# Windowed attention: queries turned raw, divided out inside the exponent; keys turned as whole numbers

## The chip, the cores and the metric

One of the cores of a Trainium2 chip runs the whole program in one launch. The metric is the device time of that launch in microseconds (us). A run of the hardware profiler gives, beside it, the span from the first to the last instruction of the program; the two differ by a little under 2 us. TensorE is called PE here, its weight loads PEld, VectorE DVE, ScalarE ACT, GpSimd POOL, and the engine that issues DMAs SP.

## The reference, cut to what matters

One encoder layer is computed for 1280 tokens (1024 of one request, 256 of another) of width 2048: a norm, a wide projection, three groups of heads side by side (a two-way state space scan, a windowed attention, a cross attention to a memory), and an output projection. The change lies in the windowed attention alone. It has eight query heads of 64, two key heads, blocks of 128 tokens, and a window of one block to either side:

```python
q = rms_norm(q.reshape(b, T, ATT_HEADS, ATT_HEAD_DIM), q_norm_g)
k = rms_norm(k.reshape(b, T, ATT_KV_HEADS, ATT_HEAD_DIM), k_norm_g)
...
s = jnp.einsum('bnqgrd,bnkgd->bngrqk', qb, kw).astype(jnp.float32) * (d ** -0.5)
...
logits = jnp.where(valid[:, None, None], s - slopes[None, :, :, None, None] * dist[:, None, None], -jnp.inf)
sk = sink.astype(jnp.float32).reshape(KV, r)[:, :, None, None]
m = jnp.maximum(jnp.max(logits, axis=-1, keepdims=True), sk)
pr = jnp.exp(logits - m)
probs = pr / (jnp.sum(pr, axis=-1, keepdims=True) + jnp.exp(sk - m))
o = jnp.einsum('bngrqk,bnkgd->bnqgrd', probs.astype(v.dtype), vw)
```

The norm of a query divides a whole row of logits by one positive number. With r the reciprocal root of a query's mean square, exp(r*s - slope*dist - m) is the same as exp(r*(s - (slope/r)*dist) - m).

## The kernel before, in words

**Precision.** Every large matmul takes its operands in fp32r. A number x is split in two, a high part h that ACT writes by a copy into an fp32r tile, and a low part x - h that DVE writes. Three matmuls (h·h, h·l, l·h) then stand for one. These triples over 512, 288 or 320 columns (lines 254 to 256, 289 to 291, 1199 to 1201) accumulate in five PSUM banks of the pool "acc". They are called the stream here. For every tile of weights that arrives, ACT makes wh (line 202) and DVE wl (line 203).

**The lanes.** What is not in the stream (attention, scan, preparation of keys) is written as Python generators that yield after each step. They wait in two queues, lanes 0 and 1. After each k of a projection the function `pump` takes steps from both lanes at a rate given in RATES (in the second group of tokens some 1.6 steps of lane 0 and 2.5 of lane 1 for each k). The keys' `k_prep`, the windowed attention's `attn` and the cross attention's `mem_attn` are in lane 0, the scan in lane 1. A scheduler then orders the instructions of each engine by dependences and priorities; weight splits and evacuations stand ahead (`high_priority`). All steps share three PSUM banks of the pool "mix" (`psum(name)`), one after the other: a tile takes the bank of the third tile before it, and PE waits until that has been read. They also share a ring of five SBUF tiles called "wa" (`w2`).

**k_prep(t)**, ten times: a block's keys (128 tokens, two heads of 64) are loaded, normed on DVE (lines 488 and 489), split into a high and a low part, each written twice side by side (lines 493 and 495), turned by four fp32r transposes (line 501), and copied out of PSUM into kT by DVE (line 504) and kL by ACT (line 505). Both halves of kT's 128 partitions hold the same high parts, and both of kL's the same low parts.

**attn(t)**, ten times: the block's queries q (128 by 512) are loaded (line 593); ACT squares them, DVE adds up per head (line 598), POOL makes r by a power of -1/2 (`rsqrt`, lines 120 and 121); DVE multiplies q by r (line 604). For each of the two key heads ACT and DVE write the four query heads' high and low parts side by side into qh (lines 610 and 611), PE turns them by four transposes (line 616), ACT copies them to a tile qT (line 618), whose partitions 0 to 63 hold the high and 64 to 127 the low parts. So one matmul with kT and one with kL (lines 632 and 633) give the logits of a head. Then, in `scores`, DVE adds the slope times the distance (line 634), takes the row's maximum with the sink (lines 637 to 641), ACT takes the exponent (line 647) and DVE divides (line 652); `turn_` turns the probabilities (line 664), `values` multiplies them with v (line 674).

`mem_attn` already turns its queries unscaled and gives r to its exponent (lines 720 to 746).

Of the kernel before, what the change touches and what calls it, by code (L numbers as in the profile page):

```python
# [10 lines left out]
F32 = mybir.dt.float32  # L11
F32R = mybir.dt.float32r
# [3 lines left out]
AF = mybir.ActivationFunctionType  # L16
ALU = mybir.AluOpType
AX = mybir.AxisListType

P = 128  # L20
# [8 lines left out]
CH, WB, RB, WA, WBB = 4, 3, 4, 5, 4  # L29
# [14 lines left out]
def hymba_encoder_kernel(  # L44
# [7 lines left out]
    V, A, G, T, S = nc.vector, nc.scalar, nc.gpsimd, nc.tensor, nc.sync  # L52
# [14 lines left out]
    sm = ctx.enter_context(tc.tile_pool(name="sm", bufs=2))  # L67
# [8 lines left out]
    def const(shape, name, dtype=F32):  # L76
        return cp.tile(shape, dtype, tag=name, name=name)
# [4 lines left out]
    def psum(name):  # L82
        return mix.tile([P, 512], F32, tag="mix", name=name)


    identr = const([P, P], "identr", F32R)
    ident = identr.bitcast(F32)
# [2 lines left out]
    ones = one.broadcast_to([P, P])  # L90
    mhalf = const([P, 16], "mhalf")
    V.memset(mhalf, -0.5)

    whole = rp.tile([P, 640], F32, tag="ch", name="whole", bufs=CH)[:, :P]
    make_identity(nc, whole)
# [23 lines left out]
    def rsqrt(dst, src, scale, n):  # L119
        G.tensor_scalar(out=dst, in0=src, scalar1=scale, scalar2=EPS, op0=ALU.mult, op1=ALU.add)  # L120
        G.tensor_tensor(out=dst, in0=dst, in1=mhalf[:, :n], op=ALU.pow)

    def hv(ap, n=8):
        return ap.rearrange("p (h d) -> p h d", h=n)

    def hb(ap, n, d):
        return ap.unsqueeze(2).broadcast_to([P, n, d])
# [283 lines left out]
    def w2(name):  # L411
        return mp.tile([P, 512], F32, tag="wa", name=name, bufs=WA)
# [63 lines left out]
    def k_prep(t):  # L476
        r = w2("kr")[:, :P]
        S.dma_start(r, k_d[t])
        yield
        ss = sm.tile([P, 2], F32, tag="s2", name="kss", bufs=4)  # L480
        sq = w2("ksq")[:, :P]
        A.activation(sq, r, AF.Square)
        V.reduce_sum(out=ss, in_=hv(sq, 2), axis=AX.X)
        rr = sm.tile([P, 2], F32, tag="s2", name="krr", bufs=4)
        rsqrt(rr, ss, 1.0 / 64, 2)
        yield
        r3 = hv(r, 2)
        V.tensor_mul(r3, r3, hb(rr, 2, 64))
        V.tensor_mul(r3, r3, gq.unsqueeze(1).broadcast_to([P, 2, 64]))

        kh = mp.tile([P, 4, 2, 64], F32R, tag="wa", name="kh", bufs=WA)
        for d in range(2):
            A.activation(kh[:, 0:2, d, :], r3, AF.Copy)
        for d in range(2):
            V.tensor_sub(kh[:, 2:4, d, :], r3, kh[:, 0:2, 0, :].bitcast(F32))
        yield
        yield
        ps = psum("pk")
        kf = kh.rearrange("p a b d -> p (a b d)")
        for a in range(4):  # L500
            T.transpose(ps[:, a * P:(a + 1) * P].bitcast(F32R), kf[:, a * P:(a + 1) * P], identr)
        sl = t if t < 5 else t - 3
        c = slice(sl * P, (sl + 1) * P)
        V.tensor_copy(kT[:, :, c], hv(ps[:, :256], 2))
        A.activation(kL[:, :, c], hv(ps[:, 256:], 2), AF.Copy)
        yield

    def kv_shift():
# [74 lines left out]
    def attn(t):  # L583
# [3 lines left out]
        nk = na * P  # L587
        d0 = (k0 - (t - 1)) * P
        s0 = k0 if t < 4 else k0 - 3
        grp, ti = divmod(t, 5)  # L590
        tc_ = slice(ti * P, (ti + 1) * P)
        q = w2("q")
        S.dma_start(q, q_d[t])
        yield
        sq = w2("sq")
# [2 lines left out]
        V.reduce_sum(out=ss, in_=hv(sq), axis=AX.X)  # L598
        r = sm.tile([P, 8], F32, tag="s8", name="qr", bufs=4)
        rsqrt(r, ss, 1.0 / 64, 8)  # L600
        for _ in range(3):
            yield
        q3 = hv(q)
        V.tensor_mul(q3, q3, hb(r, 8, 64))
        yield
        qT = []
        for b in range(2):
            qh = mp.tile([P, 4, 2, 64], F32R, tag="wa", name="qh", bufs=WA)
            qb = q3[:, 4 * b:4 * b + 4, :]
            A.activation(qh[:, :, 0, :], qb, AF.Copy)  # L610
            V.tensor_sub(qh[:, :, 1, :], qb, qh[:, :, 0, :].bitcast(F32))
            yield
            ps = psum("pq")
            qf = qh.rearrange("p a b d -> p (a b d)")
            for a in range(4):
                T.transpose(ps[:, a * P:(a + 1) * P].bitcast(F32R), qf[:, a * P:(a + 1) * P], identr)
            o = mp.tile([P, 512], F32R, tag="qT", name="qT", bufs=2)
            A.activation(o, ps, AF.Copy)
            qT.append(o)
        z = w2("za")  # L620
        S.dma_start(hv(z, 4), zT_d[0][grp][:, :, tc_])
        yield
        sk8 = sinkb.rearrange("p (v r) -> p r v", v=2)
        state_ = {}

        def scores(rr):
            lg = mp.tile([P, 2, 384], F32, tag="lg", name="lg", bufs=2)
            for kv in range(2):
                h = 4 * kv + rr
                ps = psum("psc")  # L630
                st = qT[kv][:, rr * P:(rr + 1) * P]
                T.matmul(ps[:, :nk], st, kT[:, kv, s0 * P:s0 * P + nk], start=True, stop=False)
                T.matmul(ps[:, :nk], st, kL[:, kv, s0 * P:s0 * P + nk], start=False, stop=True)
                V.scalar_tensor_tensor(out=lg[:, kv, :nk], in0=ndist[:, d0:d0 + nk], scalar=2.0 ** -(h + 1),
                                       in1=ps[:, :nk], op0=ALU.mult, op1=ALU.add)
            m = sm.tile([P, 2], F32, tag="m2", name="m", bufs=10)
            V.reduce_max(out=m, in_=lg[:, :, :nk], axis=AX.X)
            sk = sk8[:, rr, :]
            nm = sm.tile([P, 2], F32, tag="m2", name="nm", bufs=10)
            V.tensor_max(m, m, sk)  # L640
            V.tensor_scalar(out=nm, in0=m, scalar1=-1.0, scalar2=None, op0=ALU.mult)
            es = sm.tile([P, 2], F32, tag="m2", name="es", bufs=10)
            V.tensor_add(es, sk, nm)
            A.activation(es, es, AF.Exp)
            den = sm.tile([P, 2], F32, tag="m2", name="den", bufs=10)
            for kv in range(2):
                A.activation(lg[:, kv, :nk], lg[:, kv, :nk], AF.Exp, bias=nm[:, kv:kv + 1],
                             accum_out=den[:, kv:kv + 1])
            V.tensor_add(den, den, es)
            V.reciprocal(out=den, in_=den)  # L650
            for kv in range(2):
                V.tensor_scalar(out=lg[:, kv, :nk], in0=lg[:, kv, :nk], scalar1=den[:, kv:kv + 1], scalar2=0.5,
                                op0=ALU.mult, op1=ALU.mult)
            state_[rr] = lg
# [24 lines left out]
        scores(0)  # L679
        yield  # L680
        scores(1)
        yield
        yield
# [818 lines left out]
    mp = beside.enter_context(tc.tile_pool(name="mp", bufs=2))  # L1502
# [3 lines left out]
    kT = lconst([P, 2, 7 * P], "kT", F32R)  # L1506
    kL = lconst([P, 2, 7 * P], "kL", F32R)
# [12 lines left out]
    ndist = lconst([P, 384], "ndist", BF16)  # L1520
    gq, gm = lconst([P, 64], "gq"), state[:, :P]
    dskip, sinkb = lconst([P, 16], "dskip"), lconst([P, 8], "sinkb")
# [158 lines left out]
```

## Time and profile before

| | |
|---|---|
| runs shown | 1801.31, 1802.39 and 1802.70 us, median 1802.39 |
| the profiled execution, its own time | 1802.42 us |
| its span | 1800.7 us |
| PE busy | 1791.2 us, 10546 matmuls |
| DVE, ACT, POOL busy | 1244.3, 903.0 and 439.5 us |
| granted TensorE clock | 1.00 |
| first and last turning of queries | 552.5 and 1317.0 us |

PE is at work nearly throughout. "Busy" counts a matmul from its start to its modelled end, and neighbours overlap: a 128x512 matmul of the stream is listed with some 0.39 us, while the next one starts 0.23 us after it. What a matmul costs the program is the time from its start to the next one's start, and a view in order of time gives that.

### The profile page before, as it was taken

How to read it: one execution, taken by the hardware profiler on the slowest of the kernel's cores; microseconds unless marked ns; L12 is line 12 of the kernel's file. 1: busy time of each engine (PE TensorE's matmuls, PEld its weight loads, DVE VectorE, ACT ScalarE, POOL GpSimd, SP SyncE). 2: the span in 40 equal slices, each digit the busy share in tenths (PEclk: the TensorE clock that was granted, in tenths of full speed). 3: DMA queues.
4: the chain of work that ended last, by engine and by line, in shares of the span. 5: the costliest groups of instructions: out<-in, count | busy, mean ns of one | idle time of the engine just before them, and what ended most of it. 6: DMA issues, size and time to landing. Idle time of an engine off the chain costs nothing.

```text
span 1800.7 us, 30423 instructions
## 1 busy us (share of the span) xinstructions
PE 1791.2 (99%) x10546; PEld 1606.1 (89%) x10546; DVE 1244.3 (69%) x2422; ACT 903.0 (50%) x2039; POOL 439.5 (24%) x714
## 2 busy tenths in 40 slices
PE   9999999999999999999999999999999999999999
PEld 7789999999887899999989987887898888889999
DVE  5595788877657978775755866666885654866665
ACT  6554455444445756564435646544574533543332
POOL 0105789961110000000000000001100000058775
PEclk9999999999999999999999999999999999999999
DMA  8664455446544644444436355457785564644442
GB/s 291 198 179 120 138 153 146 129 136 218 164 136 147 184 134 140 121 132 134 119 96 192 110 161 180 128 178 235 231 266 168 184 190 138 216 153 147 142 143 80
DMA packets 198891, 290.58 MB, mean 161 GB/s; under 512 B 18960, under 2 KB 80464, under 8 KB 198736
## 3 DMA queue, kind: packets, MB, share of 16 engines
q1 hardware_dynamic: 198592, 288.57, 52.7%
q8 instruction: 83, 1.36, 0.3%
q14 instruction: 72, 0.59, 0.1%
q10 hardware_dynamic: 144, 0.06, 0.0%
HBM read 231.12 MB, written 57.44 MB: 160 GB/s over the span
## 4 chain that ended last, share of the span: by engine, by line
PE 61%; DVE 1%; ACT 1%; issue 1%; DMA 1%; POOL 0%; POOLq 0%; ACTq 0%; DVEq 0%
PE acc L254 9%; PE acc L256 8%; PE acc L255 8%; PE acc L289 5%; PE acc L291 5%; PE acc L290 5%; PE acc L1199 3%; PE acc L1201 3%; PE acc L1200 3%; PE py L931 2%; PE po L674 1%; PE ppt L664 1%; PE accm L1200 1%; PE accm L1201 1%; PE accm L1199 1%
## 5 line engine op out<-in xcount | busy, mean ns | idle before, releaser
L203 DVE TENSOR_TENSOR wl<-wraw,wh 128x512 fp32r<-128x512 f32 (+1 forms) x480 | 338.9, 708 | 241.3 <-ACT wh L202 230.7
L254 PE MATMUL acc<-wh,xH 128*128 128x512 f32 (+1 forms) x1248 | 481.9, 386 | 0.2 <-ACT mkr L416 0.2
L255 PE MATMUL acc<-wl,xH 128*128 128x512 f32 (+1 forms) x1248 | 472.2, 378 | 0.9 <-DVE wl L203 0.6
L256 PE MATMUL acc<-wh,xL 128*128 128x512 f32 (+1 forms) x1248 | 472.8, 379 | 0.0
L202 ACT ACTIVATE wh<-wraw 128x512 fp32r<-128x512 f32 (+1 forms) x480 | 292.4, 613 | 323.5 <-PE acc L256 173.3
L254 PEld LDWEIGHTS acc<-wh,xH 128*128 128x128 f32 x1248 | 234.5, 188 | 45.1 <-issue 4.8
L255 PEld LDWEIGHTS acc<-wl,xH 128*128 128x128 f32 x1248 | 234.7, 188 | 43.8 <-DVE wl L203 3.3
L256 PEld LDWEIGHTS acc<-wh,xL 128*128 128x128 f32 x1248 | 234.2, 188 | 43.9 <-issue 0.9
L289 PE MATMUL acc<-xH,wh 128*128 128x320 f32 x640 | 204.5, 320 | 0.0
L291 PE MATMUL acc<-xH,wl 128*128 128x320 f32 x640 | 198.6, 310 | 0.0
L290 PE MATMUL acc<-xL,wh 128*128 128x320 f32 x640 | 198.3, 310 | 0.0
L203 DVE TENSOR_TENSOR sl<-ws,sh 128x384 fp32r<-128x384 f32 x144 | 99.6, 695 | 96.9 <-ACT sh L202 96.6
L202 ACT ACTIVATE sh<-ws 128x384 fp32r<-128x384 f32 x144 | 74.6, 523 | 176.5 <-POOL ws L1171 81.5
L1171 POOL TENSOR_TENSOR ws<-wraw 128x128 f32<-128x128 f32 x144 | 91.1, 633 | 202.0 <-DMA wraw<-in_w_in_pairs_dram 83.6
L289 PEld LDWEIGHTS acc<-xH,wh 128*128 128x128 f32 x640 | 120.3, 188 | 4.1 <-issue 3.7
L290 PEld LDWEIGHTS acc<-xL,wh 128*128 128x128 f32 x640 | 120.3, 188 | 2.6 <-issue 2.2
L291 PEld LDWEIGHTS acc<-xH,wl 128*128 128x128 f32 x640 | 120.1, 188 | 0.7 <-issue 0.6
L1171 POOL TENSOR_TENSOR ws<-wraw,ws 128x128 f32<-128x128 f32 x144 | 93.5, 649 | 11.3
L358 DVE SCALAR_TENSOR_TENSOR c<-u,vec,c 128x638 f32<-128x638 f32 (+1 forms) x96 | 88.6, 926 | 10.0 <-ACT c L353 9.7
L1171 POOL TENSOR_TENSOR ws<-ws,wraw 128x128 f32<-128x128 f32 x144 | 94.2, 654 | 0.0
L120 POOL TENSOR_SCALAR qr<-qss 128x8 f32<-128x8 f32 x10 | 4.3, 428 | 366.6 <-DVE qss L598 366.6
L1171 POOL TENSOR_TENSOR wraw<-wraw 128x128 f32<-128x128 f32 x144 | 89.2, 620 | 11.1
(427 smaller groups left out, 3645.1 us busy)
## 6 DMA issues: line engine op xcount, KB each, us to landing
wraw<-in_w_in_laid_dram SPq DMA_DIRECT2D x208, 256.0 KB, 2.8
wraw<-in_w_in_pairs_dram SPq DMA_DIRECT2D x80, 256.0 KB, 2.8
wraw<-in_w_out_laid_dram SPq DMA_DIRECT2D x64, 256.0 KB, 3.5
wraw<-in_w_out_pairs_dram SPq DMA_DIRECT2D x64, 256.0 KB, 2.8
rf<-ac SPq DMA_DIRECT2D x40, 256.0 KB, 3.7
rb<-ac SPq DMA_DIRECT2D x40, 256.0 KB, 4.1
wraw<-in_w_mem_laid_dram SPq DMA_DIRECT2D x32, 256.0 KB, 4.8
xst<-in_x_sample_dram SPq DMA_DIRECT2D x20, 256.0 KB, 4.7
```

The lines of the kernel that those rows point to most:

```text
L202: a = A.activation(h, raw, AF.Copy)
L203: b = V.tensor_sub(l, raw, h.bitcast(F32))
L254: T.matmul(ps[t][:, :n], sh, h[:, :n], start=(k_ == 0), stop=False)
L255: T.matmul(ps[t][:, :n], sh, l[:, :n], start=False, stop=False)
L256: T.matmul(ps[t][:, :n], sl, h[:, :n], start=False, stop=(k_ == KT - 1))
L289: T.matmul(o, sh, cur["H", q][:, m, c], start=(k == 0), stop=False)
L290: T.matmul(o, sh, cur["L", q][:, m, c], start=False, stop=False)
L291: T.matmul(o, sl, cur["H", q][:, m, c], start=False, stop=(k == KT - 1))
L358: V.scalar_tensor_tensor(out=c[0], in0=u[:, k:k + n], scalar=cw[k], in1=c[0], op0=ALU.mult, op1=ALU.add)
L1171: G.tensor_tensor(out=o, in0=x, in1=y, op=op)
L1199: T.matmul(ps[p], h, xh, start=(k_ == 0), stop=False)
L1200: T.matmul(ps[p], h, xl, start=False, stop=False)
```

## The change

Keys: the normed block is written twice side by side in fp32 and turned by two transposes in fp32, not split before. DVE then copies the high part out of PSUM into kT and subtracts it from PSUM into kL; ACT's copy into kL is gone.

Queries: the raw block is turned as it was loaded, four transposes instead of eight. Each now holds two neighbouring heads, the even one in partitions 0 to 63, the odd one in 64 to 127. For either half ACT copies the high part into a tile qT at the same partitions, and DVE writes the low part into the other half of that tile. The multiplication by r is gone. In its place DVE makes 1/r, slope/r and sink/r (three instructions of 8 columns), the slope of line 634 becomes a column, the maximum is multiplied by -r, and the exponent's scale is r, a column too. A constant tile of eight slopes is set at the start by eight memsets.

`attn` now yields nine times ahead of its first scores, and eight times before: 22 steps in all against 21. `k_prep` has as many as it had.

```diff
+    slope = const([P, 8], "slope")
+    for h in range(8):
+        V.memset(slope[:, h:h + 1], 2.0 ** -(h + 1))
...
-        kh = mp.tile([P, 4, 2, 64], F32R, tag="wa", name="kh", bufs=WA)
+        k2 = mp.tile([P, 2, 2, 64], F32, tag="wa", name="k2", bufs=WA)
         for d in range(2):
-            A.activation(kh[:, 0:2, d, :], r3, AF.Copy)
-        for d in range(2):
-            V.tensor_sub(kh[:, 2:4, d, :], r3, kh[:, 0:2, 0, :].bitcast(F32))
+            A.activation(k2[:, :, d, :], r3, AF.Copy)
         yield
         yield
         ps = psum("pk")
-        kf = kh.rearrange("p a b d -> p (a b d)")
-        for a in range(4):
-            T.transpose(ps[:, a * P:(a + 1) * P].bitcast(F32R), kf[:, a * P:(a + 1) * P], identr)
+        for a in range(2):
+            T.transpose(ps[:, a * P:(a + 1) * P], k2[:, a].rearrange("p d c -> p (d c)"), ident)
...
         V.tensor_copy(kT[:, :, c], hv(ps[:, :256], 2))
-        A.activation(kL[:, :, c], hv(ps[:, 256:], 2), AF.Copy)
+        V.tensor_sub(kL[:, :, c], hv(ps[:, :256], 2), kT[:, :, c].bitcast(F32))
...
-        q = w2("q")
+        qr = mp.tile([P, 512], F32R, tag="wa", name="q", bufs=WA)
+        q = qr.bitcast(F32)
...
         rsqrt(r, ss, 1.0 / 64, 8)
-        for _ in range(3):
+        yield
+        yield
+        ps = psum("pq")
+        for a in range(4):
+            T.transpose(ps[:, a * P:(a + 1) * P].bitcast(F32R), qr[:, a * P:(a + 1) * P], identr)
+
+        qT = [mp.tile([P, 512], F32R, tag="qT", name="qT", bufs=2) for _ in range(2)]
+        for b in range(2):
+            x, y = slice(64 * b, 64 * b + 64), slice(64 - 64 * b, 128 - 64 * b)
+            A.activation(qT[b][x], ps[x], AF.Copy)
+            V.tensor_sub(qT[b][y], ps[x], qT[b][x].bitcast(F32))
             yield
-        q3 = hv(q)
-        V.tensor_mul(q3, q3, hb(r, 8, 64))
-        yield
-        qT = []
-        for b in range(2):
-            qh = mp.tile([P, 4, 2, 64], F32R, tag="wa", name="qh", bufs=WA)
-            qb = q3[:, 4 * b:4 * b + 4, :]
-            A.activation(qh[:, :, 0, :], qb, AF.Copy)
-            V.tensor_sub(qh[:, :, 1, :], qb, qh[:, :, 0, :].bitcast(F32))
-            yield
-            ps = psum("pq")
-            qf = qh.rearrange("p a b d -> p (a b d)")
-            for a in range(4):
-                T.transpose(ps[:, a * P:(a + 1) * P].bitcast(F32R), qf[:, a * P:(a + 1) * P], identr)
-            o = mp.tile([P, 512], F32R, tag="qT", name="qT", bufs=2)
-            A.activation(o, ps, AF.Copy)
-            qT.append(o)
+        yield
+
+        ri = sm.tile([P, 8], F32, tag="s8", name="qri", bufs=4)
+        V.reciprocal(out=ri, in_=r)
+        slr, skr = [sm.tile([P, 8], F32, tag=n, name=n, bufs=1) for n in ("slr", "skr")]
+        V.tensor_mul(slr, ri, slope)
+        V.tensor_mul(skr, ri, sinkb)
+        yield
+        yield
...
-                st = qT[kv][:, rr * P:(rr + 1) * P]
+                st = qT[rr % 2][:, h // 2 * P:(h // 2 + 1) * P]
...
-                V.scalar_tensor_tensor(out=lg[:, kv, :nk], in0=ndist[:, d0:d0 + nk], scalar=2.0 ** -(h + 1),
+                V.scalar_tensor_tensor(out=lg[:, kv, :nk], in0=ndist[:, d0:d0 + nk], scalar=slr[:, h:h + 1],
...
-            V.tensor_max(m, m, sk)
-            V.tensor_scalar(out=nm, in0=m, scalar1=-1.0, scalar2=None, op0=ALU.mult)
+            V.tensor_max(m, m, skr8[:, rr, :])
+            V.scalar_tensor_tensor(out=nm, in0=m, scalar=-1.0, in1=r8[:, rr, :], op0=ALU.mult, op1=ALU.mult)
...
-                A.activation(lg[:, kv, :nk], lg[:, kv, :nk], AF.Exp, bias=nm[:, kv:kv + 1],
+                h = 4 * kv + rr
+                A.activation(lg[:, kv, :nk], lg[:, kv, :nk], AF.Exp, scale=r[:, h:h + 1], bias=nm[:, kv:kv + 1],
```

How the instructions move. Line numbers of the changed program are three to four higher than before. The first place is PE's order at the first block's queries, before (L616 turns qh into the bank pq, L254 to L256 are the stream):

```order
L255 MATMUL acc<-wl,xH_1178 128x512
L256 MATMUL acc<-wh,xL_1179 128x512
L616 MATMUL pq<-identr,qh 128x128 x8
L254 MATMUL acc<-wh,xH_859 128x512
L255 MATMUL acc<-wl,xH_859 128x512
```

The same place of the changed program (L606 turns q, L935 is a matmul of the scan in lane 1, L257 to L259 are the stream):

```order
L259 MATMUL acc<-wh,xL_1188 128x512
L935 MATMUL py<-xs,rb 128x64 x8
L606 MATMUL pq<-identr,q 128x128 x4
L257 MATMUL acc<-wh,xH_1187 128x512
L258 MATMUL acc<-wl,xH_1187 128x512
```

Two groups of four have become one, it comes some 28 rows earlier, and here it follows another short group directly.

The second place is DVE's order at the same block, before (qss is the sum of squares from which POOL makes qr; wl is the low part of a weight tile; ya and zs belong to other work):

```order
L598 TENSOR_REDUCE qss<-sq 128x8
L203 TENSOR_TENSOR wl<-wraw,wh 128x512
L934 TENSOR_TENSOR ya<-xs,dco 128x512
L504 CAST kT<-pk 128x2x128
L203 TENSOR_TENSOR wl<-wraw,wh 128x512 x2
L604 TENSOR_TENSOR q<-q,qr 128x512
L611 TENSOR_TENSOR qh<-q,qh 128x4x64 x2
L203 TENSOR_TENSOR wl<-wraw,wh 128x512
```

and now:

```order
L599 TENSOR_REDUCE qss<-sq 128x8
L206 TENSOR_TENSOR wl<-wraw,wh 128x512
L938 TENSOR_TENSOR ya<-xs,dco 128x512
L504 CAST kT<-pk 128x2x128
L206 TENSOR_TENSOR wl<-wraw,wh 128x512
L505 TENSOR_TENSOR kL<-pk,kT 128x2x128
L206 TENSOR_TENSOR wl<-wraw,wh 128x512
L617 RECIPROCAL qri<-qr 128x8
L619 TENSOR_TENSOR slr<-qri,slope 128x8
L620 TENSOR_TENSOR skr<-qri,sinkb 128x8
L206 TENSOR_TENSOR wl<-wraw,wh 128x512
L941 TENSOR_TENSOR ya<-ya,py 128x512
```

The first instruction that needs POOL's qr is now the reciprocal, six instructions behind the sum instead of five; the two subtractions out of pq follow a few rows further on.

The third place is PE's order at the queries of the ninth block (t = 8), with the buffers' numbers. Before, right behind the two groups of transposes and thirty matmuls of the stream (psc is a head's logits, pyb a matmul of the scan's way back):

```order
L632 MATMUL psc_14383<-kT_4805,qT_14295 128x256
L633 MATMUL psc_14383<-kL_4806,qT_14295 128x256
L632 MATMUL psc_14387<-kT_4805,qT_14320 128x256
L633 MATMUL psc_14387<-kL_4806,qT_14320 128x256
L1029 MATMUL pyb_14408<-state_4813,cc_14301 128x512
L632 MATMUL psc_14418<-kT_4805,qT_14295 128x256
L633 MATMUL psc_14418<-kL_4806,qT_14295 128x256
L632 MATMUL psc_14422<-kT_4805,qT_14320 128x256
L633 MATMUL psc_14422<-kL_4806,qT_14320 128x256
```

and now, at the transposes themselves (pr is a turning of the scan's output, L292 to L294 the stream):

```order
L606 MATMUL pq_14295<-identr_84,q_14172 128x128 x4
L1033 MATMUL pyb_14308<-state_4822,cc_14224 128x512
L997 MATMUL pr_14317<-identr_84,yd_14092 128x128 x4
L292 MATMUL acc_14346<-xH0_6769,wh_14352 128x320
L293 MATMUL acc_14346<-xL0_6770,wh_14352 128x320
L294 MATMUL acc_14346<-xH0_6769,wl_14353 128x320
L292 MATMUL acc_14347<-xH0_6769,wh_14352 128x320
L293 MATMUL acc_14347<-xL0_6770,wh_14352 128x320
L1033 MATMUL pyb_14325<-state_4822,cc_14224 128x512
```

Before, five tiles of the pool "mix" followed one another directly at the scores; now pyb_14325 is the third tile behind pq_14295, so it takes pq's bank, five matmuls of the stream behind pr.

More of the change, by code (lines that the diff above doesn't have):

```diff
@@ L622, in attn @@
         yield
-        sk8 = sinkb.rearrange("p (v r) -> p r v", v=2)
+        sk8, skr8, r8 = [x.rearrange("p (v r) -> p r v", v=2) for x in (sinkb, skr, r)]
         state_ = {}
```

## The prediction

> **What bounds the kernel now.** I read the page first: the busy shares, then the chain that ended last.
>
> ```profile
> span 1800.7 us, 30423 instructions
> ...
> PE 1791.2 (99%) x10546; PEld 1606.1 (89%) x10546; DVE 1244.3 (69%) x2422; ACT 903.0 (50%) x2039; POOL 439.5 (24%) x714
> ...
> PE 61%; DVE 1%; ACT 1%; issue 1%; DMA 1%; POOL 0%; POOLq 0%; ACTq 0%; DVEq 0%
> ```
>
> PE is idle for 9.5 us of 1800.7, and no other engine has more than 1% of the chain. To see whether that also holds where the windowed attention runs (queries are turned from 552 to 1317 us), I cut the span in three.
>
> ```profile
> 0.00:480.00 480.00, 477.14 (x2796) 438.91 (x2797) 348.85 (x576) 242.59 (x480) 229.95 (x367) 1.00 0.56 170
> 480.00:1360.00 880.00, 878.00 (x5221) 770.43 (x5220) 628.78 (x1387) 480.30 (x1206) 50.53 (x77) 1.00 0.53 160
> 1360.00:1801.00 441.00, 436.05 (x2532) 396.73 (x2531) 266.69 (x460) 180.07 (x356) 159.02 (x270) 1.00 0.50 154
> ```
>
> The columns are the stretch, its length, then PE, PEld, DVE, ACT and POOL busy, the granted clock, the DMAs. In the middle stretch PE is idle for 2.0 us of 880, DVE for 251, ACT for 400. So there the end is moved by two things: matmul time added or taken away, and any new wait of PE. Work on DVE, ACT and POOL counts only if PE comes to wait for it.
>
> **Turned queries.** What a short group costs is the time from its start until the stream has its pace again. PE in order of time at the first queries, then at a key block, then at a turning of the memory's keys, which is one in fp32:
>
> ```profile
> 552.50 0.80 PE L616 MATMUL pq<-identr,qh 128*128 128x128 f32 x8
> 553.13 0.47 PE L254 MATMUL acc<-wh,xH 128*128 128x512 f32 x1
> 553.44 0.40 PE L255 MATMUL acc<-wl,xH 128*128 128x512 f32 x1
> ```
> ```profile
> 494.94 0.40 PE L859 MATMUL pst<-fh,btl 128*128 128x512 f32 x1
> 495.17 0.46 PE L501 MATMUL pk<-identr,kh 128*128 128x128 f32 x4
> 495.48 0.46 PE L254 MATMUL acc<-wh,xH 128*128 128x512 f32 x1
> 495.78 0.40 PE L255 MATMUL acc<-wl,xH 128*128 128x512 f32 x1
> ```
> ```profile
> 441.35 0.60 PE L444 MATMUL pmk<-identr,mkr 128*128 128x128 f32 x4
> 441.71 0.48 PE L254 MATMUL acc<-wh,xH 128*128 128x512 f32 x1
> 442.02 0.39 PE L255 MATMUL acc<-wl,xH 128*128 128x512 f32 x1
> ```
>
> A matmul of the stream takes 0.23 us from start to start (494.94 to 495.17). From the group's start to L255's start, less that one, are 0.94 - 0.23 = 0.71 us for eight transposes in fp32r, 0.61 - 0.23 = 0.38 for four, 0.67 - 0.23 = 0.44 for four in fp32. In all three the L254 behind the group takes some 0.31 instead of 0.23, so 0.08 belongs to the break itself. In PE's order before, the 80 transposes of queries stand as four groups of eight and twelve of four: 4 x 0.71 + 12 x 0.38 = 7.4 us. Now there are ten groups of four, 3.8. **The queries give back 3.6 us.**
>
> **Turned keys.** Ten groups of four in fp32r at 0.38 become ten groups of two in fp32; half of 0.44 is 0.22. **The keys give back 10 x 0.16 = 1.6 us.** The two matmuls of a head's logits keep their number and shape.
>
> **Breaks.** With the queries read earlier, the scheduler sets other short groups side by side. Counting along PE's order, the stream is taken up again behind a transpose, a value matmul or a matmul of the scan's diagonal 143 times before and 127 times now; one of the sixteen is a pq and already counted. 15 x 0.08 = **1.2 us less.** Bounds: nothing, if the wait behind a longer group eats it, and 2.4 us, if a group's front costs as much as its back.
>
> **The start.** DVE sets eight slopes between mhalf and zero, and zero is what the first matmuls wait for.
>
> ```profile
> 0.86 0.06 DVE L89 MEMSET one<- 128x1 f32 x1 [0.86 <-PEq L1667]
> 0.90 0.07 DVE L92 MEMSET mhalf<- 128x16 f32 x1
> 0.97 0.27 DVE L1460 MEMSET zero<- 128x256 f32 x1
> ```
> ```profile
> 1.30 4.64 PE L1462 MATMUL warm<-zero 128*128 128x256 f32 x10 [1.30 <-DVE zero L1460]
> 5.37 0.84 PE L254 MATMUL acc<-wh,xH 128*128 128x512 f32 x1
> ```
>
> A memset's successor starts 0.04 to 0.07 us after it, so the ten warm-up matmuls start 0.3 to 0.6 us later, and the first of the stream is issued while they still run. **0.3 us more**, by the 128x1 row; nothing, if the first operands are as late.
>
> **The other engines.** The rows by line and shape:
>
> ```profile
> L604 DVE TENSOR_TENSOR q<-q,qr 128x512 f32<-128x512 f32 x10 | 6.9, 686 | 1.8 <-POOL qr L121 1.8
> L611 DVE TENSOR_TENSOR qh<-q,qh 128x256 fp32r<-128x256 f32 x20 | 8.1, 419 | 1.0 <-ACT qh L610 1.0
> L724 DVE TENSOR_TENSOR mql<-pmq,mqh 128x512 fp32r<-128x512 f32 x10 | 6.8, 685 | 0.9 <-ACT mqh L722 0.9
> L640 DVE TENSOR_TENSOR m<-m,sinkb 128x2 f32<-128x2 f32 x40 | 6.2, 155 | 0.2
> L495 DVE TENSOR_TENSOR kh<-kr,kh 128x128 fp32r<-128x128 f32 x20 | 4.9, 286 | 3.9 <-ACT kh L493 3.9
> L504 DVE CAST kT<-pk 128x256 fp32r<-128x256 f32 x10 | 4.2, 423 | 8.9 <-PE pk L501 8.9
> ```
> ```profile
> L618 ACT ACTIVATE qT<-pq 128x512 fp32r<-128x512 f32 x20 | 11.4, 590 | 2.8 <-PE pq L616 2.8
> L610 ACT ACTIVATE qh<-q 128x256 fp32r<-128x256 f32 x20 | 7.6, 407 | 6.0 <-DVE q L604 6.0
> L505 ACT ACTIVATE kL<-pk 128x256 fp32r<-128x256 f32 x10 | 3.8, 376 | 2.1 <-DVE kT L504 1.7
> L746 ACT ACTIVATE mpr<-pms,mm,mr 128x256 f32<-128x256 f32 x40 | 22.2, 560 | 23.0 <-DVE mm L742 23.0
> L647 ACT ACTIVATE lg<-lg,nm 128x256 f32<-128x256 f32 x32 | 16.0, 502 | 13.9 <-DVE nm L641 13.9
> ```
>
> DVE, for a query block: 0.69 + 2 x 0.42 = 1.52 go; two subtractions of 512 columns out of PSUM come (0.685 each, L724 is the like) and three of 8 columns at 0.155: 1.84. For a key block two of 0.286 go, one like L504 at 0.42 comes. Over ten blocks +3.2 and -1.5: 1.7 us more, under DVE's 251 idle ones. ACT loses 20 x 0.407 and 3.8 us. Its exponent takes r as a column; L746, which has that already, takes 560 ns for 256 columns where L647 takes 502, though it reads PSUM: 80 x 0.058 = 4.6 us more. In sum ACT has 7.3 us less. All of it is covered by PE, at nothing.
>
> For that column the Trainium skill, ScalarE: Activation LUTs, section What ACT_TABLE_LOAD costs, has a price that speaks against the change: each [128,1] pointer operand adds about 93 ns to an ACTIVATE. By it the exponents would grow by an estimated 7.4 us instead of 4.6; the rows' 58 ns compare two sources, so this trace neither confirms nor excludes 93.
>
> The reciprocal waits for POOL's qr. Behind it on DVE stand weight splits, for which the stream waits. In DVE's order six instructions lie between the sum and it, five before, so the 1.8 us that L604 waited in all ten blocks do not grow. Ready queries come five steps before their scores and no longer one: PE's weight loads waited 1.5 us for qT and PE itself 0.2, and I take the **0.2 as gain**, 1.5 at most.
>
> ```profile
> PE psc L632 <- ACT qT L618: 0.2, 1, 0.2
> ...
> PE ppt L664 <- DVE lg L652: 0.9, 2, 0.5
> ```
> ```profile
> PEld psc L632 <- ACT qT L618: 1.5, 4, 0.6
> ```
>
> Queries' loads keep their number and SP its stream of weight loads; with four tiles of the "wa" ring to a block in place of six, no load finds its tile taken for longer. The added step of attn pushes lane 0 back by up to six k. The lane still empties in the same loop, and the scan's last step is the last to end in both, and the added step holds no instruction of its own, so it costs nothing.
>
> **The bank pq.** Before, one ACT copy (0.59 us) freed it. Now ACT, DVE beside ACT, DVE must have read it: 0.59 + 0.69 + 0.69 = 2.0 us at least. PE feels it only when the third tile of the pool "mix" comes within that time. The closest is the ninth block, with two pyb matmuls, pr and five of the stream between: some 2 us by the chain's rows.
>
> ```profile
> 1304.69 0.86 PE pyb L1029 x2
> ```
>
> The bounds are nothing and ten times the added 1.4, 14 us. mem_attn reads its bank by ACT and DVE already, and no row of PE's waits has more than 1.3 us. I take **0.5 us more**.
>
> **Sum**: -3.6 - 1.6 - 1.2 + 0.3 - 0.2 + 0.5 = -5.8 us. The profiled execution took 1802.42 (span and 1.7 around it), the median is 1802.39. **Forecast 1796.6 us.** A measurement of this kernel tells 0.2% from no change, 3.6 us: faster is below 1798.8, slower above 1806.0.
>
> **Rivals.**
> First, a longer chain behind the scores: with 58 ns more in both exponents of all 40 pairs of heads, `turn_` finds its probabilities later, and PE waits at ppt. If PE took all of it, 4.6 us: 1801.2, no change to be told. For it speaks that PE does wait for lg (0.9 us above); against it that these are two waits out of 80.
> The skill's 93 ns would make this rival's time an estimated 1804.0, no change either.
> Second, the other side: the bank pq. If subtractions queue behind evacuations and splits on DVE, the bank is held longer in every block, in-order PE stops, and the stream behind it. From 0.94 us a block it is slower by over 0.2%; with 1.4 us in each, instead of the 0.5 in all, 1796.6 + 13.5 = 1810.1. For it: three banks for two lanes. Against it: in nine of ten blocks the third tile is further off.
> Third, more than forecast: breaks at 2.4, the 1.5 of the weight loads, no wait for pq, start hidden: -3.6 - 1.6 - 2.4 - 1.5 = -9.1, 1793.3. For it: five score tiles in a row at the ninth block are pulled apart. Against it: waits that go often reappear elsewhere.
>
> **How the numbers follow.** Forecast 0.55, first rival 0.14, second 0.09, third 0.22. The forecast's own range is 1794 to 1799.5; with the first and third rival the range is 1791.5 to 1802, and the pq case stays outside. Faster: all of the third, most of the forecast's share, little of the first: 0.72. Within 0.2%: 0.19. Slower: 0.09.
>
> **What would show it.** Right: PE with 60 matmuls less (10486), its busy time down by some 5 us and its idle time still near 9.5; L606 as ten groups with 0.38 us each; pk as ten groups with 0.22; ACT with 7 us less, DVE about as before. Wrong: rows of PE waiting for DVE qT or ACT qT (second rival), or for DVE lg (first); a pk group that costs as much in fp32 with two as with four before would take 1.6 us of the sum; a subtraction into the other 64 partitions well over 0.7 us would lengthen the hold of pq.

## The result, and the profile after

| | before | after |
|---|---|---|
| median of 11 runs each, us | 1802.70 (1801.25 to 1806.17) | 1806.67 (1804.74 to 1809.44) |
| ratio, 95% interval | | 1.0021 [1.0013, 1.0029] |
| the profiled execution, its own time, us | 1802.42 | 1806.20 |
| PE idle in the span, us | 9.5 | 15.6 |

The changed kernel is 4 us slower, where 5.8 us less were forecast. The page of the profile after, its span, its busy shares and the chain that ended last:

```profile
span 1804.3 us, 30282 instructions
...
PE 1788.7 (99%) x10486; PEld 1602.8 (89%) x10486; DVE 1256.7 (70%) x2440; ACT 898.4 (50%) x2009; POOL 434.6 (24%) x714
...
PE 84%; DMA 5%; issue 5%; DVE 3%; ACT 2%; SPq 1%; POOL 0%; ACTq 0%; DVEq 0%; POOLq 0%
```

PE has its 60 matmuls less and its busy time fell by 2.5 us (some 5 were forecast), but its idle time grew by 6.1. DMA, ACT and DVE had 3% of the chain before and have 10% now. What PE waited for, as engine, line, tile, releaser: us in total, times, longest:

```profile
PE ppt L668 <- DVE lg L656: 2.7, 1, 2.7
PE warm L1466 <- DVE zero L1464: 1.5, 1, 1.5
PE psc L635 <- DVE lg L637: 1.2, 1, 1.2
PE pr L997 <- ACT pT L669: 1.1, 1, 1.1
PE pst L861 <- ACT pT L669: 1.0, 1, 1.0
PE pst L861 <- ACT fh L875: 0.9, 1, 0.9
PE pst L862 <- DVE fl L883: 0.9, 1, 0.9
```

No row waits for qT, so the bank pq is not it. Six waits are new at this size; one of pst for pT, 1.0 us, ends at 1086 us, the five others, 6.8 us, lie between 1269 and 1352. Busy time by stretch there, of the kernel before and then of the changed one (the columns are those of the prediction):

```profile
1260.00:1360.00 100.00, 99.09 (x627) 87.66 (x627) 83.81 (x194) 63.62 (x164) 8.37 (x16) 1.00 0.81 249
```
```profile
1260.00:1360.00 100.00, 93.01 (x582) 82.28 (x581) 80.72 (x182) 59.38 (x148) 6.36 (x14) 1.00 0.73 230
```

PE is idle for 7.0 us of these 100 and was for 0.9. Setting the starts of the same matmul of the stream side by side in both traces, the changed kernel is 5.0 us ahead at 1293 us and 2.2 us behind at 1357 us. So the changed kernel had a lead, and lost more than that in 64 us. The lead is no measure of the gain: part of it is work of lane 0, which stands later here (by how much is counted below), that was still to be done. ACT in order of time in the changed kernel shows how (L199 splits a load of the output stage's operand, L651 is the exponent of the tenth query block; the number in brackets is the idle time before a row and what ended it):

```profile
1341.48 0.82 ACT L199 ACTIVATE xH<-chd,vec 128x640 fp32r<-128x640 f32 x1
1347.47 0.83 ACT L199 ACTIVATE xH<-chd,vec 128x640 fp32r<-128x640 f32 x1 [5.17 <-DMA chd<-oT]
...
1348.82 0.59 ACT L651 ACTIVATE lg<-lg,nm,qr 128x256 f32<-128x256 f32 x1
...
1363.45 0.59 ACT L651 ACTIVATE lg<-lg,nm,qr 128x256 f32<-128x256 f32 x1
```

and DVE and then PE right behind it (L656 divides the exponents, L668 turns them):

```profile
1350.12 0.16 DVE L653 TENSOR_TENSOR den<-den,es 128x2 f32<-128x2 f32 x1 [0.57 <-ACT lg L651]
...
1351.62 0.60 DVE L656 TENSOR_SCALAR lg<-lg,den 128x256 f32<-128x256 f32 x2
```
```profile
1348.96 0.39 PE L257 MATMUL acc<-wh,xH 128*128 128x512 f32 x1
1352.01 0.70 PE L668 MATMUL ppt<-identr,lg 128*128 128x128 f32 x4 [2.66 <-DVE lg L656]
```

The first and the last of this block's eight large exponents are shown; all eight come behind a split at which ACT stands for 5.17 us, since its load has not landed and ACT takes its instructions in order. The load is not a slow one: it was issued at 1342.24 us, when ACT was just about to come to it, and landed in 5.2 us; the twelve loads of this tile between 1300 and 1360 us have a median of 4.5 us here and 4.8 in the kernel before. DVE's den, its product and PE's turning wait in line. The four smaller waits in the stretch (psc, pr and the two pst) were not followed to their ends. In the kernel before, the same eight ran from 1321 to 1346 us, before the split that waits:

```profile
1321.37 0.51 ACT L647 ACTIVATE lg<-lg,nm 128x256 f32<-128x256 f32 x1
...
1345.68 0.50 ACT L647 ACTIVATE lg<-lg,nm 128x256 f32<-128x256 f32 x1
...
1352.18 0.83 ACT L196 ACTIVATE xH<-chd,vec 128x640 fp32r<-128x640 f32 x1 [0.86 <-DMA chd<-oT]
```

Why they came later now: counted in the program, the tenth block's 21 steps stood at the k from 333 to 354 of 383, its 22 stand at 341 to 358. Each block has one more step, which takes a turn of the lane, and the loads of the output stage's operand start at fixed k, from 339 on.

### The profile page after: what moved, and what is told of

It is laid out like the page before. It is cut to its first block, busy times and chain, and to the rows that moved or that the text cites. A ratio compares the mean times of both kernels' runs of the same rounds, so it can differ in the third digit from the quotient of the medians.

```text
span 1804.3 us, 30282 instructions
## 1 busy us (share of the span) xinstructions
PE 1788.7 (99%) x10486; PEld 1602.8 (89%) x10486; DVE 1256.7 (70%) x2440; ACT 898.4 (50%) x2009; POOL 434.6 (24%) x714
## 4 chain that ended last, share of the span: by engine, by line
PE 84%; DMA 5%; issue 5%; DVE 3%; ACT 2%; SPq 1%; POOL 0%; ACTq 0%; DVEq 0%; POOLq 0%
PE acc L257 11%; PE acc L259 11%; PE acc L258 11%; PE acc L1205 6%; PE acc L1203 6%; PE acc L1204 6%; PE acc L292 5%; PE acc L293 5%; PE acc L294 5%; PE accm L1203 2%; PE accm L1204 2%; PE accm L1205 2%; PE py L935 2%; PE po L678 1%; PE ppt L668 1%
## 5 line engine op out<-in xcount | busy, mean ns | idle before, releaser
L257 PE MATMUL acc<-wh,xH 128*128 128x512 f32 (+1 forms) x1248 | 481.4, 386 | 0.4 <-DVE v_all L336 0.4
L259 PE MATMUL acc<-wh,xL 128*128 128x512 f32 (+1 forms) x1248 | 473.3, 379 | 0.0
L257 PEld LDWEIGHTS acc<-wh,xH 128*128 128x128 f32 x1248 | 234.5, 188 | 44.7 <-issue 3.2
L259 PEld LDWEIGHTS acc<-wh,xL 128*128 128x128 f32 x1248 | 234.3, 188 | 44.0 <-issue 1.3
L292 PE MATMUL acc<-xH,wh 128*128 128x320 f32 x640 | 201.5, 315 | 0.0
L294 PE MATMUL acc<-xH,wl 128*128 128x320 f32 x640 | 199.2, 311 | 0.0
L292 PEld LDWEIGHTS acc<-xH,wh 128*128 128x128 f32 x640 | 120.2, 188 | 2.4 <-issue 2.0
L294 PEld LDWEIGHTS acc<-xH,wl 128*128 128x128 f32 x640 | 120.2, 188 | 1.6 <-issue 1.6
```

The source lines that it names most:

```text
L257: T.matmul(ps[t][:, :n], sh, h[:, :n], start=(k_ == 0), stop=False)
L259: T.matmul(ps[t][:, :n], sl, h[:, :n], start=False, stop=(k_ == KT - 1))
L292: T.matmul(o, sh, cur["H", q][:, m, c], start=(k == 0), stop=False)
L294: T.matmul(o, sl, cur["H", q][:, m, c], start=False, stop=(k == KT - 1))
```

## The experiments

Three theories at first. A: the added step costs, by moving the last blocks into those loads. B: the exponents, longer by the column, hold up what follows (the prediction's first rival). C: the bank pq is held (its second).

**The step alone: taken from the change, and given to the kernel before.**

```diff
 the change
-            yield
             yield
 
         ri = sm.tile([P, 8], F32, tag="s8", name="qri", bufs=4)
```
```diff
 the kernel before
             qT.append(o)
+        yield
         z = w2("za")
```

> The changed kernel with the one yield taken out that stands alone behind the two splits of the queries, so that attn has 21 steps as before and every unit of lane 0 stands at the same k as before; all operations are the changed ones. Theory A (the added step moves the ninth and tenth block and what follows in lane 0 into the refill of the next operand, where ACT waits for that refill's loads with exponents queued behind): the stalls of PE between 1290 and 1360 us go, and the time is 1797 us, 5 to 6 below the kernel before. Theory B (the longer exponent, 88 to 92 ns more in each of 80, makes PE wait at the turned probabilities): still slower than before, near 1806. Theory C (the bank pq is held by four readers): still slower than before, 1803 to 1806.

> The kernel before with one empty yield added in attn ahead of the load of za: 22 steps, all operations as before. Theory A: slower than before by the stalls alone, 6 to 9 us, 1809 to 1812 us, with ACT waiting some 5 us for a chd load near 1345 us and PE for lg behind it. Theories B and C: as before, within 2 us of it.

Without the step 1802.25 us (11 runs), ratio to the kernel before 0.9999 [0.9991, 1.0008]: by the ratios 4.0 us less than the change, but not below the kernel before, so the 1797 that theory A gave did not come. With the step alone 1808.71 (6 runs), 1.0036 [1.0024, 1.0048]: an empty step costs 6.3 us, with no change to the work at all. Its ACT waits for the same loads, though not for 5 us at one of them as was expected; the stretch, then what ACT waited for:

```profile
1260.00:1360.00 100.00, 96.29 (x611) 86.50 (x609) 80.65 (x180) 60.12 (x152) 7.93 (x14) 0.98 0.77 241
```
```profile
ACT xH L196 <- DMA chd<-oT: 5.0, 4, 1.9
```

In the changed kernel this row reads:

```profile
ACT xH L199 <- DMA chd<-oT: 7.1, 3, 5.2
```

PE's longest wait in the kernel with the step alone is not for lg either, but for the bank pq (pst takes the bank that the copy L618 to qT has to free), and the granted clock is at half behind that wait:

```profile
PE pst L858 <- ACT qT L618: 3.5, 1, 3.5
```
```profile
1341.00:1342.00 1.00, 1.00 (x3) 0.75 (x3) 1.00 (x3) 1.00 (x3) 0.00 (x0) 0.50 0.99 218
```

The copy, at 1338.16 us, comes behind splits on ACT that stood for their loads 1.90, 0.86 and 0.52 us, and behind other work of ACT. From 1339.6 to 1343.3 us the stream's matmuls start up to 0.43 us apart and not 0.23, which loses some 1.6 us. With the 2.8 us that PE is idle more in this stretch, that is 4.4 of the 5.7 us by which the two profiled spans differ. The mean granted clock is 0.998 or 0.999 in all six runs of this kernel and 1.000 in all 29 of the kernel before beside them. In the changed kernel it is 0.999 in five of eleven runs, whose median is 1807.92 us, and 1.000 in the other six, with 1805.8. So part of the price can be a slower clock behind a wait; the trace of the change, taken at 1.000, does not hold it.

**The exponent's column alone, and the keys alone, in the kernel before.** `one` is a column of ones.

```diff
-                A.activation(lg[:, kv, :nk], lg[:, kv, :nk], AF.Exp, bias=nm[:, kv:kv + 1],
+                A.activation(lg[:, kv, :nk], lg[:, kv, :nk], AF.Exp, scale=one, bias=nm[:, kv:kv + 1],
```

> The kernel before, whose 80 exponents of the windowed attention take a column of ones as their scale in place of the constant 1: the output stays what it was, and each exponent reads one more column. All theories: ACT's exponents rise from 606 and 502 ns to some 698 and 590, 7 us of ACT in all. Theory B: 4 to 7 us slower than before, 1807 to 1810. Theories A and C: within 1.5 us of before.

> The kernel before with the changed preparation of the keys alone (turned in fp32 by two transposes, low part subtracted out of PSUM by DVE); queries as before. All theories: ten groups of PE at 0.22 instead of 0.38 us, 1.6 us less, 1801; the scheduler may move that by 1 us. If two fp32 transposes cost as much as four in fp32r, as before.

With the column 1802.19 (11 runs), 1.0003 [0.9994, 1.0011], and not 4 to 7 us more: theory B falls. The exponents did grow, all 80, and were covered:

```profile
L647 ACT ACTIVATE lg<-lg,nm,one 128x384 f32<-128x384 f32 x48 | 33.5, 699 | 20.1 <-DVE nm L641 20.1
L647 ACT ACTIVATE lg<-lg,nm,one 128x256 f32<-128x256 f32 x32 | 18.9, 592 | 12.2 <-DVE nm L641 12.1
```

The keys' part of the diff alone: 1800.66 (11 runs), 0.9992 [0.9983, 1.0000], 1.4 us of a forecast 1.6, with an interval from nothing to 3.1.

**Is it the step or the place?** The change keeps its step, and lane 0 gets 22/21 of its rate in the second group's projections, so that the tenth block stands at 332 to 354 again.

```diff
-         {'kv': (1.2, 1.5), 'x': (1.75, 1.85), 'q': (1.6, 2.5), 'za': (1.6, 2.5), 'z0': (1.55, 2.6),
-          'z1': (1.55, 2.65), 'mq': (1.55, 2.8), 'zm': (1.55, 2.85), 'o': (1.95, 1.9)})
+         {'kv': (1.2, 1.5), 'x': (1.75, 1.85), 'q': (1.676, 2.5), 'za': (1.676, 2.5), 'z0': (1.624, 2.6),
+          'z1': (1.624, 2.65), 'mq': (1.624, 2.8), 'zm': (1.624, 2.85), 'o': (1.95, 1.9)})
```

> The change with its added step, and with lane 0's rate 22/21 of what it was for the second group's q, za, z0, z1, mq and zm (1.676 for 1.6, 1.624 for 1.55), so that the last four blocks of the windowed attention stand at the k where they stand in the kernel before (the tenth at 332 to 354 of 383, not 341 to 358). Theory A (the step costs because it moves the tenth block's exponents into the loads of the output stage's operand): 1802.2, as the change without the step, and ACT's wait of 5 us for a chd tile near 1347 us gone. If the number of steps itself or the later places in the first group cost: 1806.7 as the change.

1798.10 us (11 runs), 0.9982 [0.9973, 0.9991]: by the ratios 7.0 us less than the change (8.6 by medians that were taken apart) for five per cent more on six rates, and 3.2 us less than the kernel before. The stretch:

```profile
1260.00:1360.00 100.00, 99.98 (x626) 88.27 (x626) 85.19 (x193) 64.64 (x162) 9.92 (x16) 1.00 0.79 250
```

and ACT at the loads, the tenth block's first and last exponent ahead of the split that waits:

```profile
1320.35 0.58 ACT L651 ACTIVATE lg<-lg,nm,qr 128x256 f32<-128x256 f32 x1
...
1342.33 0.59 ACT L651 ACTIVATE lg<-lg,nm,qr 128x256 f32<-128x256 f32 x1
...
1349.96 0.83 ACT L199 ACTIVATE xH<-chd,vec 128x640 fp32r<-128x640 f32 x1 [1.15 <-DMA chd<-oT]
```

PE's idle time fell from 7.0 to 0.02 us in the stretch where it was lost. The kernel is 4 us faster than the 1802.2 that theory A gave, for which a reason is looked for below. The time is the place's, not the step's.

**The control: the kernel before with the empty step and the same rates.**

> The kernel before with the empty step (1808.7 when it ran with the old rates) and with lane 0 faster by 22/21 in the second group: every step of attn that does the same work stands at the k at which the change with the faster lane has it, so the two differ by the change's work alone. Theory A (places cost, not the step): the 6.3 us of the empty step are gone, 1801.5 to 1803. If the forecast's terms are worth their sum, the change with the faster lane (1798.1) lies 5.8 us below, so 1804; if what the change gave there came from the places, this kernel is at 1798 to 1799 too.

1803.61 us (12 runs), 1.0000 [0.9991, 1.0009]: the empty step's 6.3 us are gone, as theory A has it, and nothing is gained beyond. So what the change gains at these places is its own work. No run moved the loads themselves: that they are what the late places run into rests on the traces.

```profile
1260.00:1360.00 100.00, 99.26 (x630) 87.63 (x629) 85.49 (x198) 64.50 (x165) 9.83 (x16) 1.00 0.81 251
```

**Fewer steps still.** The change with 20 steps, two yields less (the one taken out above and the one shown), and the slopes made late.

```diff
         V.tensor_mul(skr, ri, sinkb)
         yield
-        yield
```

> The change with two steps of attn less (20 in all) and the slopes made late: the tenth block of the windowed attention ends two k earlier than in the kernel before. Theory A allows a gain: another 0 to 2 us less than the change without the added step and with late slopes, 1799 to 1801. If the earlier places make DVE or ACT late elsewhere (queries' loads have less time ahead of their sum of squares): 1802 or more, with a new row of PE's waits.

1802.41 us (11 runs), 1.0004 [0.9995, 1.0012], with new waits of PE; earlier is no better than in place:

```profile
PE ppt L663 <- DVE lg L651: 1.8, 2, 1.6
```

**Why does the change without its step gain nothing?** At its places 1802.25, at other places 1798.10. First suspect, theory D: the new tile of slopes.

```diff
-    slope = const([P, 8], "slope")
-    for h in range(8):
-        V.memset(slope[:, h:h + 1], 2.0 ** -(h + 1))
...
     dtb, aneg = lconst([P, 32], "dtb"), lconst([P, 32], "aneg")
+    slope = lconst([P, 8], "slope")
+    for h in range(8):
+        V.memset(slope[:, h:h + 1], 2.0 ** -(h + 1))
```

> The change without the added step, and with its tile of slopes made where the windowed attention's other constants are made (behind the ten units of the first half), so that nothing stands ahead of the zero tile at the start and no tile made at the start is moved in SBUF. Theory D (the early tile of slopes costs 0.2 us at the start and, by moving other tiles, some 0.7 ns for each 320-column matmul of the stage from 150 to 405 us): the first matmul of the stream at 5.37 us again, those matmuls at 146.1 ns instead of 146.8, and 1.3 us less than the change without the added step: about 1800.9. Theory E (the gain went into late transfers and other waits that have nothing to do with the tile): 1802.2 as before, and the 320-column matmuls stay at 146.8 ns.

The other way round, the three removed lines alone were put into the kernel before:

> The kernel before with the tile of eight slopes and its eight memsets added, which nothing reads. Theory D: 1.3 us slower than the kernel before, about 1803.7, with the 320-column matmuls of 150 to 405 us at 146.8 ns instead of 146.1 and the first matmul of the stream 0.2 us later. Theory E: 0.2 us, no difference that can be told.

1802.22 (11 runs), 1.0007 [0.9998, 1.0016], and 1801.87 (11 runs), 1.0002 [0.9994, 1.0011]. Theory D falls on both: without the early tile the 320-column matmuls still took 146.8 ns, and with it alone 146.1.

Second suspect, theory G: the first group's places. Where the change with 22 steps has moved on by two to five k, the 21 steps stand as before. Stretches of the change without its step, then of the one with the step and the faster lane:

```profile
680.00:780.00 100.00, 99.43 (x686) 93.88 (x686) 79.70 (x173) 57.98 (x139) 4.81 (x6) 1.00 0.44 132
780.00:830.00 50.00, 48.11 (x334) 47.37 (x334) 32.60 (x63) 27.62 (x70) 1.90 (x3) 0.97 0.39 119
```
```profile
680.00:780.00 100.00, 99.99 (x691) 94.68 (x688) 84.00 (x184) 60.34 (x150) 3.04 (x4) 1.00 0.44 133
780.00:830.00 50.00, 50.00 (x372) 49.84 (x371) 34.36 (x66) 27.45 (x64) 2.41 (x4) 1.00 0.47 140
```

The clock of 0.97 in the first is again a half clock behind a wait, of 1.9 us at 799 us; it lasts 3.4 us and loses some 1.6:

```profile
803.00:804.00 1.00, 1.00 (x6) 1.00 (x5) 0.97 (x2) 0.60 (x1) 0.00 (x0) 0.50 0.37 109
```

In the first, PE is idle for 2.5 us, in the second for none; in the kernel before, with the places of the first, for 0.9:

```profile
680.00:780.00 100.00, 99.53 (x691) 94.26 (x690) 77.61 (x169) 56.89 (x138) 4.38 (x5) 1.00 0.44 133
780.00:830.00 50.00, 49.55 (x361) 48.92 (x360) 35.18 (x71) 30.45 (x79) 2.98 (x4) 1.00 0.44 123
```

In the change without its step DVE waits for an earlier store to give its buffer back, and a reciprocal of the cross attention stands behind it:

```profile
798.58 0.17 DVE L390 COPY u<-carry 128x4 f32<-128x4 f32 x1 [1.74 <-DMA xbc_d<-u]
...
799.90 0.15 DVE L751 RECIPROCAL mden<-mden 128x2 f32<-128x2 f32 x1
```

Both kernels with 21 steps got the places that the change has in the first group, by two rates:

```diff
-RATES = ({'kv': (2.0, 1.0), 'mq': (2.4, 1.6), 'z0': (2.2, 1.7), 'z1': (2.2, 1.7)},
+RATES = ({'kv': (2.0, 1.0), 'mq': (2.292, 1.6), 'z0': (2.101, 1.7), 'z1': (2.2, 1.7)},
```

> The kernel before, with lane 0's rates in the first group's mq and z0 at 0.955 of what they were (2.292 and 2.101), so that the third and fourth blocks of the windowed attention and the cross attention's first five stand one to four k later, as they do in the change, and everything from the sixth block on stands as before. Theory G (the first group's places in the kernel before cost a wait for a late transfer near 799 us, of 0.6 to 2 us, and another 1 to 2 us between 700 and 760 us; the change moves past them): 1799 to 1800, with no row of PE waiting for DVE mpr. Theory H (the places of the first group are worth nothing in themselves): 1802.

> The change without its added step (1802.2 when it ran before), with the same rates of 0.955 in the first group's mq and z0. Theory G: 1798, as the change with its step and the faster lane in the second group, with no wait near 799 us. Theory H: 1802, so that it would be the second group in which the two differ.

The kernel before: 1802.73 (11 runs), 1.0003 [0.9994, 1.0013]. The change without its step: 1798.51 (11 runs), 0.9981 [0.9972, 0.9990]. So G holds for the change and H for the kernel before: the old places cost the change 3.7 us by the medians, 3.2 ± 2.2 by the ratios, and cost the kernel before nothing on balance. The wait near 799 us is gone in both:

```profile
780.00:830.00 50.00, 50.00 (x372) 49.85 (x371) 33.14 (x64) 28.11 (x67) 2.41 (x4) 1.00 0.48 140
```

**The tiles.** slr and skr, too, are moved behind the windowed attention's constants, in the change with the faster lane and in the change without its step at the new places.

```diff
-        slr, skr = [sm.tile([P, 8], F32, tag=n, name=n, bufs=1) for n in ("slr", "skr")]
...
+    slope, slr, skr = [lconst([P, 8], n) for n in ("slope", "slr", "skr")]
```

> The change with its added step and lane 0 faster by 22/21 in the second group (1798.1 when it ran before), with slope, slr and skr all allocated behind the windowed attention's constants, so that the pool of small tiles is as large as in the kernel before. Theory F (slr and skr, two tiles more in the pool of small tiles, move the tiles that are allocated later, and the 320-column matmuls of 150 to 405 us take 146.80 ns instead of 146.12 for it): 146.1 ns again, 1668 matmuls by 0.68 ns = 1.1 us, and 0.2 us at the start: 1796.8. If the addresses have nothing to do with it: 146.8 ns, 1798.0.

> The change without its added step, with the rates of 0.955 in the first group's mq and z0 (1798.5 when it ran), and with slope, slr and skr allocated behind the windowed attention's constants. Theory F: the 320-column matmuls of 150 to 405 us at 146.1 ns again, and 1.3 us less: 1797.2. If it gains nothing: 1798.5.

1798.08 (11 runs), 0.9976 [0.9967, 0.9985], and 1797.35 (6 runs), 0.9969 [0.9958, 0.9980]. Each is 0.0006 and 0.0012 below its like, 1.1 and 2.2 us, of which neither can be told from nothing alone. The time from start to start of the 320-column matmuls, though, went back to 146.1 ns in both (rows in the last section). The last is the fastest kernel of this study: 0.9969 of 1802.39 is 1796.8 us. That is near the forecast, but for a kernel with three further edits that the forecast did not have.

## Why the prediction was wrong, point by point

**The step that failed** is this: "The added step of attn pushes lane 0 back by up to six k. [...] the added step holds no instruction of its own, so it costs nothing." It costs 6.3 us in the kernel before, and in the change 7.0 us against the same step with the faster lane, by the ratios. That it moves the lane was known (up to six k; the tenth block starts eight later), the ends of the lane were looked at (the last loop, the last step of the scan), but not what stands still while the lane moves: the loads that begin at k 339. The question that was put to other edits, which instruction queues behind which wait on an in-order engine, was not put to this one.

**The queries' 3.6 us** came. A group of transposes in the changed kernel, in order of time:

```profile
592.91 0.47 PE L606 MATMUL pq<-identr,q 128*128 128x128 f32 x4
...
593.51 0.39 PE L258 MATMUL acc<-wl,xH 128*128 128x512 f32 x1
```

0.60 less 0.23 is 0.37 us, 0.38 forecast; there are ten such groups. **The keys' 1.6** came too: 0.45 less 0.23 is 0.22, as forecast, and alone they gave 1.4 in the ratio.

```profile
495.94 0.38 PE L501 MATMUL pk<-identr,k 128*128 128x128 f32 x2
...
496.39 0.39 PE L258 MATMUL acc<-wl,xH 128*128 128x512 f32 x1
```

**Breaks, start, waits, bank.** The 0.3 of the start measured 0.23 (the stream's first matmul at 5.60 and not 5.37 us). The bank cost nothing seen, 0.5 forecast. The breaks' 1.2 and the 0.2 of qT were not measured by themselves. PE's busy time speaks for less than the forecast's 5 us: between kernels at equal places it fell by 3.4 us (runs e14 and e7) and 3.6 us (e9 and e10).

**The sum** can only be held against kernels at equal places. Ratios to the kernel before, differences with half widths added as root of squares: faster lane with the change against without it (e7, e14) -0.0018 ± 0.0013, which is -3.2 ± 2.3 us; slower mq and z0 (e10, e9, run side by side) -0.0022 ± 0.0013, -4.0 ± 2.4; the latter with the tiles late (e12, e9) -0.0034 ± 0.0015, -6.1 ± 2.7. The forecast -5.8 lacked a loss that only the first two carry, some 1.1 us by the tiles; -4.7 then lies in both, and -5.8 in the third. But a fourth pair at equal places, the change without its step (e1) against the kernel before, gives -0.0001 ± 0.0009, -0.2 ± 1.6 us, and there the sum is not found. So the terms are borne out at the places of three pairs, within wide intervals, and at the old places something else took the gain.

**DVE and ACT** were mis-sized, and no wait of PE in these traces is put down to that. ACT's busy time fell by 4.6 us (7.3 forecast), and DVE's rose by 12.4 (1.7 forecast). Exponents and logits by line and shape in the changed kernel:

```profile
L651 ACT ACTIVATE lg<-lg,nm,qr 128x384 f32<-128x384 f32 x48 | 33.5, 698 | 4.9 <-DVE nm L644 4.6
L637 DVE SCALAR_TENSOR_TENSOR lg<-ndist,slr,psc 128x384 f32<-128x384 bf16 x48 | 27.7, 609 | 5.0 <-PE psc L636 4.9
L651 ACT ACTIVATE lg<-lg,nm,qr 128x256 f32<-128x256 f32 x32 | 18.9, 590 | 10.0 <-DVE nm L644 9.9
...
L612 DVE TENSOR_TENSOR qT<-pq,qT 64x512 fp32r<-64x512 f32 x20 | 13.8, 689 | 4.9 <-ACT qT L611 4.3
```

And the same lines before:

```profile
L647 ACT ACTIVATE lg<-lg,nm 128x384 f32<-128x384 f32 x48 | 29.1, 606 | 21.8 <-DVE nm L641 21.7
L634 DVE SCALAR_TENSOR_TENSOR lg<-ndist,psc 128x384 f32<-128x384 bf16 x48 | 25.2, 548 | 8.2 <-PE psc L633 8.2
```

The exponent's column costs 92 ns at 384 columns and 88 at 256 (502 before), not 58, 7.2 us in place of 4.6. The Trainium skill, ScalarE: Activation LUTs, section What ACT_TABLE_LOAD costs, has about 93 ns for a pointer operand, and this trace agrees. That the slope became a column was not costed at all: 61 ns for each of these 48 on DVE, 2.5 us. The rest of DVE's 12.4 was not followed. The subtraction into the other partitions takes 689 ns, 685 forecast.

**The rivals.** None of the three happened: the exponent's column alone costs nothing, and no matmul waits for qT. The kernel was slower by a mechanism that was in the text, priced at nothing. The step's price of 6.3 and the terms' -4.7 would make 1804.0; measured were 1806.7. By the ratios it is 1.8 us more than the kernel before against 3.8 measured; the intervals of the three numbers make some ± 3.5 us, so that the step costs more in the change than alone is not shown.

**Open also:** why the change without its step loses at the old places what the kernel before does not. The store behind the DVE wait near 799 us landed later there: the copy that it held ran at 798.58, and at 797.56 without a wait in the kernel before. Between its profiled execution (1804.04 us) and that with the slower mq and z0 (1800.14) the two stretches hold all of the 3.9 us: 2.3 of idle time and 1.6 of half clock. But the first is the only one of its eleven runs with a mean clock under 1.000 and lies 1.8 us above their median, so what the other runs lose is not shown.

## What to carry to other kernels

A step that is empty still moves everything behind it in its lane; look at what does not move with it (loads started at fixed points, and the in-order engine that must wait for them) before it is put down as free. To hold an edit's own worth against its forecast, give the kernel before the same places: without the two controls the change would have been thrown away for its transposes, which did all that they should. Where the number of steps must change, the lane's rate has to go with it. And look at the granted clock behind a wait of the bounding engine, not only at the wait.

## What had not been expected of the hardware

The same 320-column matmuls have two paces, by where two small tiles, slr and skr, are allocated. Three hundred of them in a row, first and last start, in the changed kernel:

```profile
207.11 0.31 PE L1204 MATMUL accm<-tL,wh 128*128 128x320 f32 x1
...
251.14 0.31 PE L1204 MATMUL acc<-xL,wh 128*128 128x320 f32 x1
```

and in the change with the faster lane and all three tiles late:

```profile
208.37 0.31 PE L1200 MATMUL accm<-tL,wh 128*128 128x320 f32 x1
...
252.20 0.31 PE L1200 MATMUL acc<-xL,wh 128*128 128x320 f32 x1
```

44.03 us make 146.8 ns each, 43.83 make 146.1. All kernels with slr and skr in the pool of small tiles had the first, the others the second, over some 1670 matmuls: 1.1 us. No program line differs in that stage. Which address matters was not looked for.

A wait of PE can be followed by a half clock. Behind waits of 1.9 us (the change without its step, at 799 us) and 3.5 us (the step alone, at 1335 us) the granted clock was 0.50 for 3.4 us. Behind the 2.7 us of the changed kernel, at 1349 us, it stayed at 1.00. What decides between the two was not found.
